# Seven products of halves in place of eight in the second product of the last dense layer

## Chip, core and metric

The kernel runs on one core of one Trainium2 chip. The metric is the device time of one execution in microseconds, the median of several runs; smaller is better. The engines are named as in the profile: PE is TensorE (matrix products, with PEld for the load of the stationary operand), DVE is VectorE, ACT is ScalarE, POOL is GpSimd, and SP is SyncE, which only issues DMAs here.

## What is computed

A trunk of two pre-norm residual layers over 512 tokens of width 1024, in float32. The first layer mixes tokens with a gated MLP over chunks, the second with multi-scale retention. Each is followed by a dense layer with squared ReLU, and a last RMSNorm ends the trunk. What matters here is the dense layer behind the second mixer and the norm at the end:

```python
h = rmsnorm(x, norm_ffn_g[i])
a = jax.nn.relu(h @ w1)            # 512 x 1024 times 1024 x 4096
x = x + (a * a) @ w2               # 512 x 4096 times 4096 x 1024
...
return rmsnorm(x, final_norm_g)
```

## The kernel before

**Precision.** Every float32 operand of a product is split in two fp32r parts, a high part (a cast, by ScalarE) and a low part (operand minus high part, by VectorE). A product is then three matmuls: high x high, high x low, low x high. `mm3` (L213 to L217) issues them; a line of it stands for matmuls of many places, so the profile's rows are told apart by their tiles: `up` is the first product of a dense layer, `dt` the second product of the last layer, `dn` that of the first.

**Weights.** `pieces_f` and `pieces_t` cut a weight matrix into raw tiles of 1 MB (`Raw`), each of which gives two pieces (`Piece`). `load_raws` (L160) issues the loads on SP into one of two raw buffers, `prep` (L172) splits a piece: ScalarE casts it to `wH` (L179, 4 buffers), VectorE subtracts to `wL` (L183, 3 buffers).

**Order.** The program is written out by hand: each engine executes its instructions in the order in which the code issues them (`manual_schedule`), and semaphores between engines follow from the tiles. `step` appends a step and the pieces that it uses to a list. At the end the list is run; each step issues its matmuls, then `advance` (the next part of unfinished evacuations, which are generators in `pending`), then `refill` (L199): high parts up to 3 pieces ahead of the step, low parts up to 2. Then come what the step has been given to do `behind` it and its own evacuation.

**Buffers.** A pool `bigp` of 10 buffers of 8 KB a partition holds the large activations. PSUM has 6 banks `acc` and 2 banks `mis`. The residual `xT` (features x tokens, 8 tiles) and the split normalised activations `hH`, `hL` have tiles of their own.

**The last dense layer.** The hidden width of 4096 is cut in four blocks q of 1024. `up(1, q)` (L641) computes one block of the first product in 8 steps (`feat`, L312), each 128 hidden features x 512 tokens, 8 row chunks x 3 = 24 matmuls with 512 columns. Its evacuation `evac_a` (L621) makes Relu and its square on ScalarE, and from them the split activations `aH`, `aL`. The norm's factor per token is not applied to the activations; its square, `r2`, is applied later. `down_t(q)` (L920) multiplies one block with w2: for each half c of the 1024 output columns four steps (`tokens`, L339), each 4 token tiles x 2 row chunks x 3 = 24 matmuls, accumulated in four PSUM banks over the block. `evac_last` (L861) adds a bank times `r2` to `xtok`, the residual with tokens on the partitions, which `to_tokens` (L847) makes by transposes during `up(1, 0)`. For the last block, `ends` (L897) goes token tile by token tile, so that the final norm and the stores (`finish`, L873) overlap. The order is up 0, gain load, up 1, down 0, up 2, down 1, up 3, down 2, down 3; `load_gain` (L929) loads the last norm's gain into `wide` and scales it.

**The norm ahead of it.** `norm` (L294) sums squares over features with a matmul by ones and forms the inverse root `r4` (`stats`); with `wide=True` it also spreads the factor over the partitions, by two more matmuls (`spread`, L281, rows `bc`), into `rbc`. The last layer's norm has `wide=False` before.

Of the kernel before, what the change touches and what calls it, by code (L numbers as in the profile page):

```python
# [32 lines left out]
class Raw:  # L33


    def __init__(self, src, parts=1):
        self.src, self.parts, self.tile, self.done = src, parts, None, 0


class Piece:  # L40
# [38 lines left out]
def trunk(ctx, tc, x, norm_mix_g, norm_ffn_g, a_w_in, a_b_in, a_v_norm_g, a_w_s, a_b_s, a_w_out,  # L79
          b_w_in, b_head_norm_g, b_w_out, mlp_w1, mlp_w2, final_norm_g, trig, decay, out):  # L80
    nc = tc.nc
    ctx.enter_context(tc.manual_schedule())

    keep = ctx.enter_context(tc.tile_pool(name="keep", bufs=1))
    wts = ctx.enter_context(tc.tile_pool(name="wts", bufs=3))
    bigp = ctx.enter_context(tc.tile_pool(name="bigp", bufs=10))
    work = ctx.enter_context(tc.tile_pool(name="work", bufs=2))
    psum = ctx.enter_context(tc.tile_pool(name="psum", bufs=6, space=PSUM))

    RAW_BUFS, LOOK = 2, 3  # L90

    def big(shape, dt, name):
        return bigp.tile(shape, dt, tag="big", name=name)

    def tmp(name, tag, bufs=2):
        return work.tile([P, T], F32, tag=tag, name=name, bufs=bufs)

    def zt(name):
        return tmp(name, "z", 4)
# [4 lines left out]
    def acc(name):  # L104
        return psum.tile([P, 512], F32, tag="acc", name=name, bufs=6)
# [4 lines left out]
    def f32(ap):  # L110
        return ap.bitcast(F32)
# [7 lines left out]
    wide = keep.tile([P, D], F32, name="wide")  # L119
    rbc, r2bc = wide[:, 0:T], wide[:, T:D]  # L120
# [7 lines left out]
    ms0 = keep.tile([P, NT], F32, name="ms0")  # L128

    keep.tile([P, 320], F32, name="fill")  # L130
    xT = [keep.tile([P, T], F32, name=f"xT{k}") for k in range(KD)]
    hH = [keep.tile([P, T], F32R, name=f"hH{k}") for k in range(KD)]
    hL = [keep.tile([P, T], F32R, name=f"hL{k}") for k in range(KD)]
    make_identity(nc, ident)
# [14 lines left out]
    order, steps, raws, pending = [], [], [], []  # L149
    pos = {"raw": 0, "piece": 0, "low": 0, "done": 0}  # L150

    def load_part(r):
        if r.tile is None:
            r.tile = wts.tile([P] + list(r.src.shape[1:]), F32, tag="raw", name=f"raw{raws.index(r)}", bufs=RAW_BUFS)
        s = r.src.shape[1] // r.parts
        i = r.done
        nc.sync.dma_start(out=r.tile[:, i * s : (i + 1) * s, :], in_=r.src[:, i * s : (i + 1) * s, :])
        r.done += 1

    def load_raws(upto):  # L160
        while pos["raw"] < min(upto, len(raws)):
            r = raws[pos["raw"]]
            while r.done < r.parts:
                load_part(r)
            pos["raw"] += 1

    def prep_tiles(i):
        p = order[i]
        p.hi = wts.tile(p.shape, F32R, tag="wH", name=f"wH{i}", bufs=4)
        p.lo = wts.tile(p.shape, F32R, tag="wL", name=f"wL{i}", bufs=3)  # L170

    def prep(upto, low=None):  # L172

        low = upto if low is None else low
        while pos["piece"] < min(upto, len(order)):
            p = order[pos["piece"]]
            load_raws(raws.index(p.raw) + RAW_BUFS)
            prep_tiles(pos["piece"])
            nc.scalar.copy(out=p.hi, in_=p.raw.tile[p.view])  # L179
            pos["piece"] += 1  # L180
        while pos["low"] < min(low, len(order)):
            p = order[pos["low"]]
            nc.vector.tensor_sub(out=p.lo, in0=p.raw.tile[p.view], in1=f32(p.hi))  # L183
            pos["low"] += 1

    def launch(g):
        if next(g, "end") != "end":
            pending.append(g)

    def advance():  # L190
        for g in list(pending):
            if next(g, "end") == "end":
                pending.remove(g)
# [5 lines left out]
    def refill():  # L199
        n = pos["done"]  # L200
        prep(n + (LOOK if n >= 4 else 1), n + (LOOK - 1 if n >= 4 else 1))

    def step(fn, *ps):
        for p in ps:
            order.append(p)
            if p.raw not in raws:
                raws.append(p.raw)
        steps.append((fn, ps))

    def do(fn):  # L210
        step(lambda: fn())

    def mm3(ps, ah, al, bh, bl, start, stop):  # L213

        nc.tensor.matmul(ps, lhsT=ah, rhs=bh, start=start, stop=False)  # L215
        nc.tensor.matmul(ps, lhsT=ah, rhs=bl, start=False, stop=False)  # L216
        nc.tensor.matmul(ps, lhsT=al, rhs=bh, start=False, stop=stop)  # L217


    state = {}  # L220
# [73 lines left out]
    def norm(name, wide=True, square=False):  # L294

        yield from stats(state["ssq"], r4, 1.0 / D, name)
        if wide:
            yield from spread(r4, rbc, name)
            if square:
                nc.scalar.activation(r2bc, rbc, AF.Square)  # L300


    def mm_f(p, ps, bH, bL, ks, last):
        for k in ks:
            mm3(ps, p.hi[:, k, :], p.lo[:, k, :], bH[k], bL[k], k == 0, k == last)
# [6 lines left out]
    def feat(p, bufs, evac, name, behind=None):  # L312

        def run(p):
            ps = acc(name)
# [211 lines left out]
    def nxt(g, times=1):  # L527
        return lambda: [next(g, None) for _ in range(times)]
# [92 lines left out]
    def evac_a(q, i):  # L621
        def ev(ps):
            b = 2 * q + i // 4
            if i % 4 == 0:
                aH[b] = big([P, 4, T], F32R, f"aH{q}_{i}")
                aL[b] = big([P, 4, T], F32R, f"aL{q}_{i}")
            h, l = aH[b][:, i % 4, :], aL[b][:, i % 4, :]
            r, s = zt(f"r{i}"), z2t(f"rr{i}")
            nc.scalar.activation(r, ps, AF.Relu)  # L629
            nc.scalar.activation(s, r, AF.Square)  # L630
            nc.vector.tensor_mul(h, r, r)  # L631
            yield
            nc.vector.tensor_sub(out=l, in0=s, in1=f32(h))
        return ev
# [210 lines left out]
    xtok = [None, None]  # L845

    def to_tokens(c, n):  # L847
        if n == 0:
            xtok[c] = big([P, NT, 512], F32, f"xtok{c}")
        ps = mis(f"tt{c}{n}")  # L850
        for k in range(4):
            nc.tensor.transpose(ps[:, k * P : (k + 1) * P], xT[4 * c + k][:, n * P : (n + 1) * P], ident)
        nc.scalar.copy(out=xtok[c][:, n, :], in_=ps)

    nrm_f1 = norm("ffn1", wide=False)

    def s2():
        next(nrm_f1, None)
        nc.vector.tensor_mul(r2, r4, r4)
# [67 lines left out]
    up(1, 0, {i: (lambda v=v, i=i: ([to_tokens(*a) for a in v], next(nrm_f1) if i == 2 else s2() if i == 3 else None)) for i, v in tt.items()}, late=True)  # L927

    def load_gain():  # L929
        nc.sync.dma_start(out=wide, in_=final_norm_g.partition_broadcast(P))  # L930
        nc.vector.tensor_scalar_mul(wide, wide, 0.125)

    do(load_gain)
    up(1, 1)
    down_t(0)
    up(1, 2)
    down_t(1)
    up(1, 3)
    down_t(2)
    down_t(3)  # L940


# [18 lines left out]
    for k in range(2):  # L961
        p = order[0]
# [56 lines left out]
```

## Time and profile before

| | |
|---|---|
| median of 3 runs | 1407.23 us (1405.75 to 1407.27) |
| the profiled execution's own time | 1407.72 us |
| its span, first to last instruction | 1406.0 us |
| PE busy | 1390.5 us, 6290 matmuls |
| DVE busy | 793.0 us, 1102 instructions |
| ACT busy | 507.2 us, 721 instructions |
| POOL busy | 127.7 us, 98 instructions |
| moved by DMA | 135.23 MB, mean 96 GB/s |
| mean granted PE clock | 0.998 |
| first matmul of the last dense layer | about 1043 us |
| last matmul of the kernel starts | 1395.26 us |

In a row of groups stand line, engine, operation, tiles out<-in and shape, the count, the busy time in us and the mean of one in ns, and behind the second bar the idle time of that engine just before these instructions, with what ended it. In a row of waits stand the waiting engine, tile and line, what released it, and the total, the number of times and the longest, in us. In a row of the timeline stand start and duration in us, and in square brackets the idle time before with its releaser.

### The profile page before, as it was taken

How to read it: one execution, taken by the hardware profiler on the slowest of the kernel's cores; microseconds unless marked ns; L12 is line 12 of the kernel's file. 1: busy time of each engine (PE TensorE's matmuls, PEld its weight loads, DVE VectorE, ACT ScalarE, POOL GpSimd, SP SyncE). 2: the span in 40 equal slices, each digit the busy share in tenths (PEclk: the TensorE clock that was granted, in tenths of full speed). 3: DMA queues.
4: the chain of work that ended last, by engine and by line, in shares of the span. 5: the costliest groups of instructions: out<-in, count | busy, mean ns of one | idle time of the engine just before them, and what ended most of it. 6: DMA issues, size and time to landing. Idle time of an engine off the chain costs nothing.

```text
span 1406.0 us, 15372 instructions
## 1 busy us (share of the span) xinstructions
PE 1390.5 (99%) x6290; PEld 1155.4 (82%) x6290; DVE 793.0 (56%) x1102; ACT 507.2 (36%) x721; POOL 127.7 (9%) x98
## 2 busy tenths in 40 slices
PE   8999999999999999999999999999999999999997
PEld 7888888888888888888888888888888888888885
DVE  6757765775444445476647574564685443434335
ACT  4656633334413223123334323333334422313222
POOL 3010111220000000011111100110130000000002
PEclk9999999999999999999999999999999999999999
DMA  6332222232223322423222131132122332232221
GB/s 225 109 116 90 72 90 88 81 120 90 90 90 104 106 90 90 148 89 108 90 78 72 60 120 60 62 118 90 61 90 91 120 104 90 93 117 91 90 90 60
DMA packets 106101, 135.23 MB, mean 96 GB/s; under 512 B 2400, under 2 KB 79792, under 8 KB 105776
## 3 DMA queue, kind: packets, MB, share of 16 engines
q1 hardware_dynamic: 106000, 134.26, 29.4%
q8 instruction: 49, 0.80, 0.2%
q14 instruction: 20, 0.16, 0.0%
q10 hardware_dynamic: 32, 0.01, 0.0%
HBM read 132.16 MB, written 2.10 MB: 95 GB/s over the span
## 4 chain that ended last, share of the span: by engine, by line
PE 96%; DVE 3%; POOL 0%; ACT 0%; DMA 0%; issue 0%; SPq 0%; ACTq 0%; DVEq 0%
PE up L217 8%; PE up L216 8%; PE up L215 8%; PE dn L217 4%; PE dn L216 4%; PE dn L215 4%; PE dt L216 4%; PE dt L217 4%; PE dt L215 4%; PE g L215 2%; PE qk L215 2%; PE vv L216 2%; PE g L216 2%; PE vv L215 2%; PE g L217 2%; PE vv L217 2%
## 5 line engine op out<-in xcount | busy, mean ns | idle before, releaser
L183 DVE TENSOR_TENSOR wL<-raw,wH 128x1024 fp32r<-128x1024 f32 x239 | 305.9, 1282 | 112.8 <-PE dt L216 65.5
L179 ACT CAST wH<-raw 128x1024 fp32r<-128x1024 f32 x239 | 249.7, 1045 | 264.7 <-PE dt L217 114.9
L215 PE MATMUL up<-hH,wH 128*128 128x512 f32 x480 | 187.2, 390 | 0.0
L217 PE MATMUL up<-hH,wL 128*128 128x512 f32 x480 | 186.8, 389 | 0.0
L216 PE MATMUL up<-hL,wH 128*128 128x512 f32 x480 | 186.8, 389 | 0.0
L631 DVE TENSOR_TENSOR aH<-r 128x512 fp32r<-128x512 f32 x64 | 45.0, 703 | 159.5 <-ACT r L629 159.4
L216 PEld LDWEIGHTS up<-hL,wH 128*128 128x128 f32 x480 | 90.1, 188 | 18.7
L215 PEld LDWEIGHTS up<-hH,wH 128*128 128x128 f32 x480 | 90.1, 188 | 18.7
L217 PEld LDWEIGHTS up<-hH,wL 128*128 128x128 f32 x480 | 90.1, 188 | 18.7
L215 PE MATMUL dn<-aH,wH 128*128 128x512 f32 x256 | 99.6, 389 | 0.0
L216 PE MATMUL dn<-aL,wH 128*128 128x512 f32 x256 | 99.6, 389 | 0.0
L217 PE MATMUL dn<-aH,wL 128*128 128x512 f32 x256 | 99.6, 389 | 0.0
L215 PE MATMUL dt<-wH,aH 128*128 128x512 f32 x256 | 99.6, 389 | 0.0
L216 PE MATMUL dt<-wL,aH 128*128 128x512 f32 x256 | 99.6, 389 | 0.0
L217 PE MATMUL dt<-wH,aL 128*128 128x512 f32 x256 | 99.6, 389 | 0.0
L629 ACT ACTIVATE r<-up 128x512 f32<-128x512 f32 x60 | 35.9, 598 | 166.7 <-PE up L217 166.7
L239 POOL TENSOR_TENSOR ssq<-ssq,sq 128x512 f32<-128x512 f32 x28 | 43.0, 1537 | 401.6 <-ACT sq L238 401.3
L501 DVE TENSOR_TENSOR xs<-dn,wide 128x512 f32<-128x512 f32 x32 | 22.1, 692 | 74.5 <-PE dn L217 74.5
L215 PEld LDWEIGHTS dt<-wH,aH 128*128 128x128 f32 x256 | 48.0, 188 | 10.1
L216 PEld LDWEIGHTS dn<-aL,wH 128*128 128x128 f32 x256 | 48.0, 188 | 10.0
L215 PEld LDWEIGHTS dn<-aH,wH 128*128 128x128 f32 x256 | 48.0, 188 | 10.0
L216 PEld LDWEIGHTS dt<-wL,aH 128*128 128x128 f32 x256 | 48.0, 188 | 9.9
(271 smaller groups left out, 2709.5 us busy)
## 6 DMA issues: line engine op xcount, KB each, us to landing
raw<-in_mlp_w_dram SPq DMA_DIRECT2D x64, 1024.0 KB, 5.1
raw<-in_b_w_in_dram SPq DMA_DIRECT2D x24, 1024.0 KB, 5.0
raw<-in_a_w_in_dram SPq DMA_DIRECT2D x14, 1024.0 KB, 5.2
raw<-in_a_w_out_dram SPq DMA_DIRECT2D x8, 1024.0 KB, 4.9
raw<-in_b_w_out_dram SPq DMA_DIRECT2D x8, 1024.0 KB, 4.9
raw<-in_a_w_in_dram SPq DMA_DIRECT2D x8, 256.0 KB, 6.7
out_dram<-out SPq DMA_DIRECT2D x8, 256.0 KB, 2.1
xr<-in_x_dram SPq DMA_DIRECT2D x3, 512.0 KB, 6.6
```

What stands on the lines that cost most here:

```text
L179: nc.scalar.copy(out=p.hi, in_=p.raw.tile[p.view])
L183: nc.vector.tensor_sub(out=p.lo, in0=p.raw.tile[p.view], in1=f32(p.hi))
L215: nc.tensor.matmul(ps, lhsT=ah, rhs=bh, start=start, stop=False)
L216: nc.tensor.matmul(ps, lhsT=ah, rhs=bl, start=False, stop=False)
L217: nc.tensor.matmul(ps, lhsT=al, rhs=bh, start=False, stop=stop)
L239: nc.gpsimd.tensor_tensor(out=state["ssq"], in0=state["ssq"], in1=sq, op=ALU.add)
L501: nc.vector.tensor_mul(t, ps, r2bc)
L629: nc.scalar.activation(r, ps, AF.Relu)
L631: nc.vector.tensor_mul(h, r, r)
```

## The change

The second product of blocks 0, 1 and 2 is done by seven products of halves (Strassen's scheme) in place of eight. With A the block's activations (512 tokens x 1024 features) and W its weights (1024 x 1024), both are cut into 2 x 2 quarters. Each of the seven products multiplies a quarter of A, or a sum of quarters (256 tokens x 512 features), with a quarter of W, or a sum of quarters (512 x 512). Its two token tiles are added to or subtracted from quarters of `xtok`, by VectorE straight from PSUM; where a product belongs to two quarters of the result, its bank is not cleared and the next product is accumulated on top (`BANK`, `FIRST`, `OUT`).

- `evac_n` replaces `evac_a` for these blocks: the factor `rbc` is applied before the square (so the norm has `wide=True`, and evacuations before the factor is there wait with Relu alone), and one float32 tile `aF` is kept unsplit.
- `make(s)` forms the activations' sum for product s where there is one (VectorE, into temporary tiles), casts it (ScalarE) and makes the low part (VectorE), into a tile `sp`. It is issued behind the first step of product s - 1.
- Sums of weights are formed by DMA: the first quarter is loaded on SP, and POOL issues a DMA that adds another quarter to the tile (`accum_op`). Three of the sums share one tile, `t1`, `t2`, `t4`: the next quarter is added when both pieces of the sum before are split (`over`, `split`). Per block that is 5 loads and 4 accumulating DMAs of 1 MB, where before there were 4 loads.
- The products of block q stand between the steps of `up` of block q + 1: one step of 24 matmuls, then one product (two steps of 12 matmuls). These `up` steps use the banks `mis`, the products the six banks `acc`.
- `load_gain` moves behind the last `up`, since `rbc` lies in `wide`. Block 3 keeps `down_t(3)`.
- Raw tiles and the residual move into `bigp`, which has 14 buffers now; loads run 2 raw tiles ahead as before, and 4 from the last dense layer on.

```diff
-    def __init__(self, src, parts=1):
+    def __init__(self, src, parts=1, adds=(), over=None):
         self.src, self.parts, self.tile, self.done = src, parts, None, 0
+        self.adds, self.over, self.split = adds, over, 0
...
-    bigp = ctx.enter_context(tc.tile_pool(name="bigp", bufs=10))
+    bigp = ctx.enter_context(tc.tile_pool(name="bigp", bufs=14))
...
-    RAW_BUFS, LOOK = 2, 3
+    LOOK = 3
+    ahead = {"raws": 2}
...
-    xT = [keep.tile([P, T], F32, name=f"xT{k}") for k in range(KD)]
+    xT2 = [big([P, 4, T], F32, f"xT{b}") for b in range(2)]
+    xT = [xT2[k // 4][:, k % 4, :] for k in range(KD)]
...
-            r.tile = wts.tile([P] + list(r.src.shape[1:]), F32, tag="raw", name=f"raw{raws.index(r)}", bufs=RAW_BUFS)
+            r.tile = big([P] + list(r.src.shape[1:]), F32, f"raw{raws.index(r)}")
...
             r = raws[pos["raw"]]
+            if r.over is not None:
+                if r.over.split < 2:
+                    return
+                r.tile, r.done = r.over.tile, r.parts
             while r.done < r.parts:
                 load_part(r)
+            for src in r.adds:
+                nc.gpsimd.dma_start(out=r.tile, in_=src, accum_op=ALU.add)
...
-            load_raws(raws.index(p.raw) + RAW_BUFS)
+            load_raws(raws.index(p.raw) + ahead["raws"])
...
             nc.vector.tensor_sub(out=p.lo, in0=p.raw.tile[p.view], in1=f32(p.hi))
+            p.raw.split += 1
             pos["low"] += 1
+            load_raws(raws.index(p.raw) + ahead["raws"])
...
-    nrm_f1 = norm("ffn1", wide=False)
+    nrm_f1 = norm("ffn1")
...
+    def evac_n(q, i):
+        def ev(ps):
+            b = 2 * q + i // 4
+            if i % 4 == 0:
+                aF[b] = big([P, 4, T], F32, f"aF{q}_{i}")
+            a = aF[b][:, i % 4, :]
+            if "rbc" in state:
+                r = zt(f"r{i}")
+                nc.vector.scalar_tensor_tensor(out=r, in0=ps, scalar=0.0, in1=rbc, op0=ALU.max, op1=ALU.mult)
+                nc.scalar.activation(a, r, AF.Square)
+                return
+            nc.scalar.activation(a, ps, AF.Relu)
+            while "rbc" not in state:
+                yield
+            nc.vector.tensor_mul(a, a, rbc)
+            nc.scalar.activation(a, a, AF.Square)
+            yield
+        return ev
+
+    def seven(q):
...
+        t1 = Raw(part(0, 0), adds=[part(0, 1)])
+        t2 = Raw(part(1, 1), adds=[part(1, 1)], over=t1)
+        t4 = Raw(part(1, 0), adds=[part(1, 0)], over=t2)
+        wraws = [Raw(part(0, 0)), t1, Raw(part(1, 0)), t2, Raw(part(1, 1)), Raw(part(0, 1), adds=[part(1, 1)]), t4]
...
+        def make(s):
+            def src(c):
+                if s in (0, 2, 6):
+                    return block(*((0, lo_t), None, (1, lo_t), None, None, None, (1, hi_t))[s], c)
+                if s == 1:
+                    sums["s", c] = half(tmp(f"sa{q}{c}", "uz"))
+                    nc.vector.tensor_sub(out=sums["s", c], in0=block(0, hi_t, c), in1=block(1, hi_t, c))
+                elif s == 3:
+                    nc.vector.tensor_sub(out=sums["s", c], in0=sums["s", c], in1=block(0, lo_t, c))
+                elif s == 4:
+                    nc.vector.tensor_add(out=sums["s", c], in0=sums["s", c], in1=block(1, lo_t, c))
+                else:
+                    sums["d", c] = half(tmp(f"sd{q}{c}", "sq"))
+                    nc.vector.tensor_sub(out=sums["d", c], in0=block(0, lo_t, c), in1=block(0, hi_t, c))
+                    return sums["d", c]
+                return sums["s", c]
+            sp = parts[s] = big([P, 2, 4, T // 2], F32R, f"sp{q}{s}")
+            for c in range(2):
+                v = src(c)
+                hi, lo = sp[:, 0, 2 * c : 2 * c + 2, :], sp[:, 1, 2 * c : 2 * c + 2, :]
+                nc.scalar.copy(out=hi, in_=v)
+                nc.vector.tensor_sub(out=lo, in0=v, in1=f32(hi))
+
+        BANK = "acbacaa"
+        FIRST = (0, 1, 2)
...
+        def one(s, i):
+            def run(p):
...
+                for t in range(2):
+                    ts = slice(t * P, (t + 1) * P)
+                    for k in range(2):
+                        kk = 2 * i + k
+                        mm3(banks[bk][t], sp[:, 0, kk, ts], sp[:, 1, kk, ts], p.hi[:, k, :], p.lo[:, k, :], s in FIRST and kk == 0, kk == 3, True)
+                advance()
+                refill()
+                if i == 0 and s < 6:
+                    make(s + 1)
+                if i == 1:
+                    (m, n), op = OUT[s]
+                    for t in range(2):
+                        xv = xtok[n][:, 2 * m + t, :]
+                        nc.vector.tensor_tensor(out=xv, in0=xv, in1=banks[bk][t], op=op)
...
+    do(lambda: ahead.update(raws=4))
...
+    for q in range(3):
+        pl = pieces_f(mlp_w1[1], (0, D), (1024 * (q + 1), 1024 * (q + 2)))
+        first, products = seven(q)
+        do(first)
+        for i in range(8):
+            feat(pl[i], hs, evac_n(q + 1, i) if q < 2 else evac_a(3, i), f"up1{q + 1}_{i}", bank=mis)
+            if i < 7:
+                products[i]()
     do(load_gain)
-    up(1, 1)
-    down_t(0)
-    up(1, 2)
-    down_t(1)
-    up(1, 3)
-    down_t(2)
     down_t(3)
```

More of the change, by code (lines that the diff above doesn't have):

```diff
@@ L211, in do, with mm3 @@
         step(lambda: fn())
[L213 to L217, printed above, removed]
+    def mm3(ps, ah, al, bh, bl, start, stop, resumed=False):
+        for i, (a, b) in enumerate(((ah, bh), (ah, bl), (al, bh))):
+            nc.tensor.matmul(ps, lhsT=a, rhs=b, start=start and i == 0, stop=stop and i == 2, skip_group_check=resumed)
     state = {}
@@ L310, in mm_o, with feat @@
             mm3(ps, p.hi[:, k, ts], p.lo[:, k, ts], bH[:, k, :], bL[:, k, :], k == 0, k == 3)
-    def feat(p, bufs, evac, name, behind=None):
+    def feat(p, bufs, evac, name, behind=None, bank=acc):
         def run(p):
-            ps = acc(name)
+            ps = bank(name)
             mm_f(p, ps, *bufs(), range(8), 7)
@@ L924, in down_t @@
                    last=ends if q == 3 and c == 1 else None)
-    tt = {2: [(0, 0), (0, 1)], 3: [(0, 2)], 4: [(0, 3)], 5: [(1, 0)], 6: [(1, 1)], 7: [(1, 2), (1, 3)]}
-    up(1, 0, {i: (lambda v=v, i=i: ([to_tokens(*a) for a in v], next(nrm_f1) if i == 2 else s2() if i == 3 else None)) for i, v in tt.items()}, late=True)
+    aF = {}
+    def evac_n(q, i):
[16 more added lines that the diff above has]
+        return ev
@@ new lines, in seven, with part, block, half @@
+    def seven(q):
+        w = mlp_w2[1]
+        def part(i, j):
+            r, c = 1024 * q + 512 * i, 512 * j
+            return w[r : r + 512, c : c + 512].rearrange("(k p) n -> p k n", p=P)
+        t1 = Raw(part(0, 0), adds=[part(0, 1)])
+        t2 = Raw(part(1, 1), adds=[part(1, 1)], over=t1)
+        t4 = Raw(part(1, 0), adds=[part(1, 0)], over=t2)
+        wraws = [Raw(part(0, 0)), t1, Raw(part(1, 0)), t2, Raw(part(1, 1)), Raw(part(0, 1), adds=[part(1, 1)]), t4]
+        pl = [[Piece(r, (slice(None), slice(2 * i, 2 * i + 2), slice(None)), [P, 2, 512]) for i in range(2)] for r in wraws]
+        lo_t, hi_t = slice(0, T // 2), slice(T // 2, T)
+        sums, parts, banks = {}, {}, {}
+        def block(h, ts, c):
+            return aF[2 * q + h][:, 2 * c : 2 * c + 2, ts]
+        def half(v):
+            return v.rearrange("p (k t) -> p k t", t=T // 2)
+        def make(s):
[22 more added lines that the diff above has]
+        FIRST = (0, 1, 2)
+        OUT = [((0, 0), ALU.add), ((1, 1), ALU.add), ((0, 0), ALU.add), ((0, 1), ALU.subtract), ((0, 1), ALU.add), ((1, 1), ALU.subtract), ((1, 0), ALU.add)]
+        def one(s, i):
+            def run(p):
+                bk = BANK[s]
+                if i == 0 and s in FIRST:
+                    banks[bk] = [acc(f"sm{q}{bk}{t}") for t in range(2)]
+                sp = parts[s]
+                for t in range(2):
[12 more added lines that the diff above has]
+                        nc.vector.tensor_tensor(out=xv, in0=xv, in1=banks[bk][t], op=op)
+            return run
+        return (lambda: make(0)), [lambda s=s: [step(one(s, i), pl[s][i]) for i in range(2)] for s in range(7)]
@@ L929, in load_gain, with got_rbc, behind_up0 @@
+    def got_rbc():
+        next(nrm_f1, None)
+        state["rbc"] = True
+    tt = {2: [(0, 0), (0, 1)], 3: [(0, 2)], 4: [(0, 3)], 5: [(1, 0)], 6: [(1, 1)], 7: [(1, 2), (1, 3)]}
+    norms = {2: nxt(nrm_f1), 3: s2, 4: nxt(nrm_f1), 5: got_rbc}
+    def behind_up0(i):
+        for a in tt.get(i, []):
+            to_tokens(*a)
+        if i in norms:
+            norms[i]()
     def load_gain():
@@ L931, in load_gain @@
         nc.vector.tensor_scalar_mul(wide, wide, 0.125)
-    do(load_gain)
-    up(1, 1)
-    down_t(0)
-    up(1, 2)
-    down_t(1)
-    up(1, 3)
-    down_t(2)
+    pl = pieces_f(mlp_w1[1], (0, D), (0, 1024))
+    do(lambda: ahead.update(raws=4))
+    feat_late(pl[0], pl[1], (evac_n(0, 0), evac_n(0, 1)), "up10")
+    for i in range(2, 8):
+        feat(pl[i], hs, evac_n(0, i), f"up10_{i}", lambda i=i: behind_up0(i))
+    for q in range(3):
[6 more added lines that the diff above has]
+                products[i]()
+    do(load_gain)
     down_t(3)
```

## Prediction

> **What bounds the kernel now.** I read first the busy table and the shares of the chain that ended last, then the waits of TensorE over the whole span, then the last stage in the timeline.
>
> ```profile
> PE 1390.5 (99%) x6290; PEld 1155.4 (82%) x6290; DVE 793.0 (56%) x1102; ACT 507.2 (36%) x721; POOL 127.7 (9%) x98
> PE 96%; DVE 3%; POOL 0%; ACT 0%; DMA 0%; issue 0%; SPq 0%; ACTq 0%; DVEq 0%
> ```
> ```profile
> engine line waited for: us in total, times, longest us
> PE xt L397 <- DMA xr<-in_x_dram: 1.8, 1, 1.8
> PE warm L958 <- POOL ident masks.py:199: 1.4, 1, 1.4
> PE bc_h L290 <- DVE dg_h L286: 0.9, 3, 0.3
> PE st_mix L272 <- POOL st_mix L263: 0.9, 1, 0.9
> ```
>
> TensorE is busy for 1390.5 of 1406.0 us, and all its waits add up to 5.0 us, none of them in the last dense layer. The remaining 10.5 us are the tail behind its last matmul. So the time moves with the number of matmuls and their spacing, as long as nothing makes TensorE wait. The spacing, from matmuls of the second product:
>
> ```profile
> 1160.20 0.39 PE L215 MATMUL dt<-wH,aH 128*128 128x512 f32 x1
> ...
> 1162.92 0.39 PE L215 MATMUL dt<-wH,aH 128*128 128x512 f32 x1
> ```
> ```profile
> L215 PE MATMUL dt<-wH,aH 128*128 128x512 f32 x256 | 99.6, 389 | 0.0
> L215 PE MATMUL up<-hH,wH 128*128 128x512 f32 x192 | 74.8, 389 | 0.0
> ```
>
> Between the two quoted starts lie 12 matmuls in 2.72 us: 0.2267 us each (0.39 is the pipelined duration, not the cost). The groups of the window 1090:1400 show `up` and `dt` at the same 389 ns, with no idle time. A step of 24 matmuls is 5.44 us, one of 12 is 2.72 us.
>
> The other engines run ahead of TensorE in this stage:
>
> ```profile
> L183 DVE TENSOR_TENSOR wL<-raw,wH 128x1024 fp32r<-128x1024 f32 x54 | 67.1, 1242 | 79.0 <-PE dt L216 65.5 <-issue 13.5
> L179 ACT CAST wH<-raw 128x1024 fp32r<-128x1024 f32 x53 | 55.5, 1047 | 114.9 <-PE dt L217 114.9
> ```
> ```profile
> 1091.00:1180.00 89.00, 89.00 (x394) 73.67 (x394) 38.83 (x44) 28.56 (x37) 0.00 (x0) 1.00 0.34 109
> 1110.00:1120.00 10.00, 10.00 (x46) 8.29 (x45) 4.16 (x6) 3.90 (x6) 0.00 (x0) 1.00 0.33 107
> ```
>
> The weight splits wait for TensorE to free their buffers, not the other way. The second fence is the table by stretches (PE, PEld, DVE, ACT, POOL busy; clock; DMA share; GB/s): VectorE is busy for 44% of 1091:1180, ScalarE for 32%, the DMA engines for a third, POOL not at all, and the clock is full.
>
> **The matmuls.** Before, each of the three blocks is 8 steps of 24 matmuls: 192. After, it is 7 products of 2 steps, each step 2 token tiles x 2 row chunks x 3 terms = 12 matmuls: 168. Three blocks save 72 matmuls, 72 x 0.2267 = **16.3 us**. The free size stays 512, and each matmul still loads its own stationary tile, so I keep the spacing. Added are the two matmuls that spread the norm's factor (`bc`); before runs the same pair without a visible price in the first dense layer, here 2 x 0.23 = **0.5 us**, up to 0.9 if they wait as `bc_h` does. Net 15.8 us, if the rest stays hidden.
>
> **VectorE, the engine that could become the bound.** A weight split now serves 12 matmuls instead of 24, and the sums and splits of the activations come on top. The prices:
>
> ```profile
> L864 DVE SCALAR_TENSOR_TENSOR xtok<-dt,r,xtok 128x512 f32<-128x512 f32 x32 | 24.0, 750 | 20.2 <-PE dt L217 20.2
> L633 DVE TENSOR_TENSOR aL<-rr,aH 128x512 fp32r<-128x512 f32 x25 | 17.3, 693 | 2.8 <-DVE aH L631 0.5
> L629 ACT ACTIVATE r<-up 128x512 f32<-128x512 f32 x25 | 15.0, 599 | 79.4 <-PE up L217 79.4
> ```
> ```profile
> L504 DVE TENSOR_TENSOR xT<-xT,ro 128x512 f32<-128x512 f32 x3 | 2.0, 677 | 0.0
> ```
> ```profile
> L788 ACT CAST ryH<-o 128x512 fp32r<-128x512 f32 x16 | 9.8, 622 | 18.8 <-DVE o L787 18.8
> ```
>
> One step of `up` and one product form a group of 5.44 + 2 x 2.72 = 10.88 us of TensorE. VectorE's work in a heavy one (the next product needs a sum): 3 weight splits x 1.22 (the 67.1 us above without one slow split of 2.34, quoted below, over 53), the evacuation of `up` 0.75, two sums and two low parts x 0.69, two updates of `xtok` x 0.68 (L504 also adds PSUM into SBUF): 8.5 us. In program order each low part directly follows its ScalarE cast, so VectorE waits out two casts x 0.62: 9.8 of 10.88 us. Written out from the start of `up` at 0: evacuation 5.60 to 6.35 (it has to wait for the end of `up`); split of the next `up` to 7.57, due 10.88; sums, casts and low parts to 11.57, due 16.32; split of the next product's first piece to 12.79, due 16.32; updates of `xtok` to 14.15, due 16.32 in the one case where the next product uses the same bank (sixth to seventh); split of the second piece to 15.37, due 19.04. The next evacuation is ready at 16.48, so 1.1 us stay idle and the pattern repeats. The smallest margin is 2.2 us. In the third block `up` still makes split activations: the evacuation begins after Relu and is 2 x 0.69; the last split ends at 16.60 where the next evacuation can begin at 17.08, and margins are 2.1 us and more. Of the six preparations inside a block, four are heavy. The sums run over two stretches of 256 instead of one of 512, which no row shows; at 10% more it is 0.3 us a group, inside the idle 1.1. So I cost this at **nothing**; the cover is the group's TensorE time, and beyond a margin of about 2 us a delay of VectorE turns into waits of TensorE.
>
> **The accumulating DMAs.** Four per block, 1 MB each, issued by POOL; t1 = W00 + W01 is loaded, then added to, then split, and t2 and t4 are added into the same tile after its splits. No DMA of before accumulates, and none of the large ones is issued by POOL. The nearest rows:
>
> ```profile
> raw<-in_mlp_w_dram SPq DMA_DIRECT2D x64, 1024.0 KB, 5.1
> raw<-in_a_w_in_dram SPq DMA_DIRECT2D x8, 256.0 KB, 6.7
> wide<-in_final_norm_g_dram SPq DMA_DIRECT2D x1, 512.0 KB, 6.0
> ```
>
> Lower bound 5.1 us, the plain load. Upper bound 4 x 6.7 = 26.8 us, had a megabyte come as four 256 KB pieces one after another. In 1110:1120 a third of the DMA time moves 107 GB/s, so 1.05 MB streams in 1.05 / (107 / 0.33) = 3.2 us; an accumulate also has to fetch the tile, so I take 5.1 + 3.2 = 8.3 us, near the plain load, since bytes, rows and target are the same. When is it late? t2 can start when VectorE has split t1's second piece, about 2.7 us into the second `up` (13.6 us from the block's start); its product starts at 38.1, and 5.6 us go for what is queued behind the waiting ScalarE cast (1.05, then two casts x 0.62 and three sums and low parts x 0.69 of the fourth product's activations, and the split's 1.22), for which TensorE waits: 18.9 us are there. On POOL, which has no other work between the norm and the tail, t2, then W01 + W11, then t4 queue behind one another: t4 has to be ready at 65, so three in a row from 13.6 leave **17 us** for each. At 8.3 us there is twice what is needed: cost **nothing**. The DMA engines carry 9 plain loads x 3.2 and 4 accumulates x 6.4 us in a block of 81.6: 67% (plain alone would be 36%). Plain loads are issued up to four tiles ahead instead of two.
>
> **What is moved.** The gain vector's load and scaling go from the start to behind the last `up`. VectorE waits at worst 6.0 us for the load (2.0 before), and behind it stand the last low part and the split that TensorE needs 10.88 us later: nothing. The last block now begins directly behind its `up`; the chunks just evacuated are needed only in its fourth step, 16 us on: nothing. The residual tiles and the raw weights move into one pool of 14 buffers; before had 10, 2 and room for the residual, so the capacity is the same, and SP's loads wait for whichever buffer is free. TensorE's slack there is unknown: nothing, up to one step late (rival C). The tail is untouched.
>
> **Sum.** Span 1406.0 - 16.3 + 0.5 = 1390.2. The profiled run took 1407.72, 1.7 more than its span, and is 0.5 above the median 1407.23; so 1391.9 against that run, and **1391.4** against the median.
>
> **Rivals.**
>
> A, nothing waits: 1390 to 1394. For it: every due time above is met.
>
> B, POOL holds up VectorE. In the tail the two meet:
>
> ```profile
> 1376.35 1.30 POOL L869 TENSOR_TENSOR xtok<-xtok,wide 128x512 f32<-128x512 f32 x1 [0.36 <-ACT fsq L866]
> 1376.39 2.34 DVE L183 TENSOR_TENSOR wL<-raw,wH 128x1024 fp32r<-128x1024 f32 x1
> ```
> ```profile
> L420 POOL TENSOR_SCALAR ws<-ws 128x1024 f32<-128x1024 f32 x1 | 2.8, 2776 | 1.9 <-DMA ws<-in_a_b_s_dram 1.9
> ```
>
> The split took 2.34 us beside a 1.30 us POOL instruction, 1.22 elsewhere. If POOL's work for an issue does the same for d us, each of 12 accumulates costs TensorE d - 2.2 (the margin): nothing at 1.3, 0.6 at 2.8 (POOL's longest row quoted), so 7 us: 1398. At d = 3.5 the gain is gone. I give it 1394 to 1404. Against it: nothing shows that issuing a DMA behaves like a POOL addition. [...]
>
> C, the common pool delays loads:
>
> ```profile
> SPq L157 <- DVE wL L183: 311.0, 30, 12.7
> ```
>
> SP already waits for VectorE to free raw tiles, up to 12.7 us at a time in 1040:1406; a load behind a tile that TensorE frees later could leave TensorE one step short: 1391.4 + 5.4 = 1397.
>
> D, slower: the accumulates are late. Place: POOL's chain of four a block. Above 17 us each they begin to delay TensorE; at 4 x X > 81.6, X > 20.4, they set the pace; the 15.8 us are gone at X = (81.6 + 5.3) / 4 = 21.7 us. At the upper bound 26.8 the blocks take 107.2 us: 3 x 25.6 = 77 more, 1468. Against it: that is over four plain loads; for it: no row shows one.
>
> **Chances.** A 0.57; B 0.17, of which 0.02 loses the whole gain to within 0.2%; C 0.06; D 0.15, of which 0.02 near no change; 0.05 for a delay in something that I took as unaffected, slower. 0.2% (2.8 us) is about what a measurement of this kernel can tell from no change. Faster 0.57 + 0.15 + 0.06 = 0.78; within 0.2% 0.04; slower 0.13 + 0.05 = 0.18. The range 1390 to 1405 takes in A, B and C, 0.80; D is left out.
>
> **What would show it.** A: 6220 matmuls, TensorE at 0.227 us, waits of TensorE still near 5 us, VectorE 80% busy inside the blocks. B: the weight splits' mean above 1.3 us and TensorE waiting for them. C: TensorE waiting for `wL` before 1040. D: an accumulate's time to landing above 17 us, ScalarE's casts of raw waiting for a DMA, and lines of TensorE waiting in the fourth and seventh product. If the spacing of matmuls in the products is not 0.227 us, the first term is wrong: each 1% of it over the 576 + 504 matmuls of the three blocks is 2.4 us.

## The result and the profile after

The changed kernel takes 1392.24 us (median of 4 runs, 1390.86 to 1393.44) against 1406.95 us of before on the same chip: ratio 0.9897, 95% interval 0.9880 to 0.9914. The profiled execution took 1392.35 us with a span of 1390.6 us. 1391.4 was forecast, with a span of 1390.2.

The busy table and the chain's shares by engine, after:

```profile
PE 1374.3 (99%) x6220; PEld 1142.2 (82%) x6220; DVE 845.8 (61%) x1183; ACT 536.2 (39%) x764; POOL 143.8 (10%) x110
PE 95%; DVE 3%; POOL 1%; DMA 0%; ACT 0%; issue 0%; SPq 0%; ACTq 0%; DVEq 0%; POOLq 0%
```

The waits of TensorE over the whole span, after:

```profile
engine line waited for: us in total, times, longest us
PE xt L408 <- DMA xr<-in_x_dram: 1.8, 1, 1.8
PE warm L1091 <- POOL ident masks.py:199: 1.4, 1, 1.4
PE bc_h L301 <- DVE dg_h L297: 0.9, 3, 0.3
PE st_mix L283 <- POOL st_mix L274: 0.8, 1, 0.8
PE st_mix L282 <- ACT st_mix L273: 0.3, 1, 0.3
PE up L228 <- ACT xtok L864: 0.2, 1, 0.2
```

TensorE has 70 matmuls fewer and 16.2 us less of busy time. Its waits sum to 5.4 us (5.0 before), and of the last dense layer there is one of 0.2 us among them. VectorE has 53 us more to do, ScalarE 29, and none of it shows in TensorE's waits. The kernel is bound as before, by a shorter list of matmuls.

One heavy group of the first block, VectorE's timeline (start, duration, instruction, idle time before it):

```profile
1140.60 0.69 DVE L956 SCALAR_TENSOR_TENSOR r<-up,wide 128x512 f32<-128x512 f32 x1 [1.63 <-PE up L228]
1141.21 1.22 DVE L193 TENSOR_TENSOR wL<-raw,wH 128x1024 fp32r<-128x1024 f32 x1
1142.35 0.68 DVE L1003 TENSOR_TENSOR sd<-aF 128x512 f32<-128x512 f32 x1
1143.71 0.69 DVE L1012 TENSOR_TENSOR sp<-sd,sp 128x512 fp32r<-128x512 f32 x1 [0.69 <-ACT sp L1011]
1144.33 0.68 DVE L1003 TENSOR_TENSOR sd<-aF 128x512 f32<-128x512 f32 x1
1145.69 0.69 DVE L1012 TENSOR_TENSOR sp<-sd,sp 128x512 fp32r<-128x512 f32 x1 [0.69 <-ACT sp L1011]
1146.31 1.22 DVE L193 TENSOR_TENSOR wL<-raw,wH 128x1024 fp32r<-128x1024 f32 x1
1147.44 1.27 DVE L1037 TENSOR_TENSOR xtok<-xtok,sm0c 128x512 f32<-128x512 f32 x2
1148.64 1.22 DVE L193 TENSOR_TENSOR wL<-raw,wH 128x1024 fp32r<-128x1024 f32 x1
1151.48 0.69 DVE L956 SCALAR_TENSOR_TENSOR r<-up,wide 128x512 f32<-128x512 f32 x1 [1.63 <-PE up L228]
```

This is the group that the prediction wrote out by hand. From one evacuation of `up` to the next it is 10.88 us, TensorE's time; VectorE waits out two ScalarE casts at 0.69 each and at the end waits 1.63 us for TensorE. As long as that last wait is there, VectorE is not the bound.

The table by stretches, one row for each of the three blocks (PE, PEld, DVE, ACT, POOL busy; clock, DMA share, GB/s):

```profile
1090.99:1172.60 81.61, 81.37 (x360) 67.33 (x360) 52.66 (x65) 35.07 (x46) 5.14 (x4) 1.00 0.70 181
1172.60:1254.20 81.60, 81.60 (x362) 67.59 (x361) 53.36 (x66) 34.43 (x44) 5.15 (x4) 1.00 0.63 155
1254.20:1335.80 81.60, 81.60 (x362) 67.59 (x361) 57.86 (x73) 38.62 (x51) 3.87 (x3) 1.00 0.52 136
```

A block lasts 81.6 us, as worked out. The accumulating DMAs, in the table of issues (KB each, median us from issue to landing) and in that of the queues (packets, MB, share of 16 engines):

```profile
raw<-in_mlp_w_dram SPq DMA_DIRECT2D x67, 1024.0 KB, 5.2
raw<-in_mlp_w_dram POOLq DMA_DIRECT2D x12, 1024.0 KB, 8.9
```
```profile
q1 hardware_dynamic: 107584, 137.41, 29.9%
q0 software_dynamic: 6336, 12.58, 5.4%
```

An accumulate lands after 8.9 us where a plain load takes 5.2. Per MB it occupies the DMA engines for 0.054 x 1390.6 / 12.58 = 6.0 us, a load for 0.299 x 1390.6 / 137.41 = 3.0 us: twice.

### The profile page after: what moved, and what is told of

It reads as the page before. It is cut to its first block, busy times and chain, and to the rows that moved or that the text cites. A ratio compares the mean times of both kernels' runs of the same rounds, so it can differ in the third digit from the quotient of the medians.

```text
span 1390.6 us, 15387 instructions
## 1 busy us (share of the span) xinstructions
PE 1374.3 (99%) x6220; PEld 1142.2 (82%) x6220; DVE 845.8 (61%) x1183; ACT 536.2 (39%) x764; POOL 143.8 (10%) x110
## 3 DMA queue, kind: packets, MB, share of 16 engines
q1 hardware_dynamic: 107584, 137.41, 29.9%
q0 software_dynamic: 6336, 12.58, 5.4%
## 4 chain that ended last, share of the span: by engine, by line
PE 95%; DVE 3%; POOL 1%; DMA 0%; ACT 0%; issue 0%; SPq 0%; ACTq 0%; DVEq 0%; POOLq 0%
PE up L228 24%; PE dn L228 13%; PE g L228 6%; PE qk L228 6%; PE vv L228 6%; PE u L228 6%; PE o L228 6%; PE v L228 5%; PE ro L228 5%; PE dt L228 3%; PE av L228 2%; PE sm2a L228 2%; PE sm1a L228 2%; PE sm0a L228 2%; PE sc L228 1%; PE v L573 1%
## 5 line engine op out<-in xcount | busy, mean ns | idle before, releaser
L193 DVE TENSOR_TENSOR wL<-raw,wH 128x1024 fp32r<-128x1024 f32 x257 | 327.4, 1276 | 49.5 <-PE v L228 10.7
L189 ACT CAST wH<-raw 128x1024 fp32r<-128x1024 f32 x257 | 267.4, 1045 | 170.0 <-PE dn L228 101.1
L642 DVE TENSOR_TENSOR aH<-r 128x512 fp32r<-128x512 f32 x40 | 27.7, 692 | 94.5 <-ACT r L640 94.4
L250 POOL TENSOR_TENSOR ssq<-ssq,sq 128x512 f32<-128x512 f32 x28 | 43.5, 1555 | 400.8 <-ACT sq L249 400.5
L640 ACT ACTIVATE r<-up 128x512 f32<-128x512 f32 x38 | 22.7, 597 | 112.5 <-PE up L228 112.5
L228 PEld LDWEIGHTS dn<-aH,wL 128*128 128x128 f32 x256 | 48.1, 188 | 9.9
L228 PE MATMUL u<-hH,wH 128*128 128x512 f32 x128 | 50.6, 395 | 0.0
L228 PE MATMUL g<-hH,wH 128*128 128x512 f32 x128 | 50.5, 395 | 0.0
L228 PE MATMUL o<-yH,wH 128*128 128x512 f32 x128 | 50.4, 394 | 0.0
L228 PE MATMUL qk<-hH,wH 128*128 128x512 f32 x128 | 50.0, 391 | 0.0
```

What stands on the lines that cost most here:

```text
L228: nc.tensor.matmul(ps, lhsT=a, rhs=b, start=start and i == 0, stop=stop and i == 2, skip_group_check=resumed)
L250: nc.gpsimd.tensor_tensor(out=state["ssq"], in0=state["ssq"], in1=sq, op=ALU.add)
```

## The experiments

The theory: the time is the number of matmuls times 0.2267 us, and VectorE's work and the accumulates are hidden, each with a margin that can be measured. The rivals: part of the gain comes from the new order or the buffers; the accumulates or VectorE are not as well hidden as they look. All runs were compared with runs of before on their own chip, whose medians were 1406.8 to 1407.4 us; the changed kernel's 1392.24 was measured in a run of its own.

### Eight products instead of seven, all else kept

Each product takes plain quarters (activations' half, token half, column half in `USE`); one split quarter of the activations serves two products, and two products are accumulated in a bank.

```diff
-        wraws = [Raw(part(0, 0)), t1, Raw(part(1, 0)), t2, Raw(part(1, 1)), Raw(part(0, 1), adds=[part(1, 1)]), t4]
+        USE = [(0, 0, 0), (0, 0, 1), (1, 0, 0), (1, 0, 1), (0, 1, 0), (0, 1, 1), (1, 1, 0), (1, 1, 1)]
+        BANK = "ababcaca"
...
+              for r in [Raw(part(h, n)) for h, m, n in USE]]
...
-        BANK = "acbacaa"
...
-            if i < 7:
-                products[i]()
+            products[i]()
```

> The three blocks are done as eight products of quarters in place of seven: everything else of the change stays (interleaving with the steps of up, activations kept whole and split late, common buffer pool), but no sums and no accumulating DMAs. 72 matmuls more than the changed kernel, 6292 in all. Theory (the time is the count of matmuls x 0.2267 us, all else is hidden): 1392.2 + 16.3 = 1408.5 us, span 1406.9, waits of TensorE near 5 us. Rival (the interleaving or the new buffers bring part of the gain): clearly below 1406.9, the time of before.

Measured: 1408.43 us (1406.78 to 1409.72), ratio to before 1.0009 (0.9999 to 1.0018), span 1406.7, TensorE busy 1391.2 us with 6292 matmuls. 16.2 us are given back, to the forecast within 0.1. The order, the late split and the norm's spread factor bring nothing; the count brings all.

### Two blocks instead of three

```diff
-    for q in range(3):
+    for q in range(2):
...
-            feat(pl[i], hs, evac_n(q + 1, i) if q < 2 else evac_a(3, i), f"up1{q + 1}_{i}", bank=mis)
+            feat(pl[i], hs, evac_n(q + 1, i) if q < 1 else evac_a(2, i), f"up1{q + 1}_{i}", bank=mis)
...
     do(load_gain)
+    up(1, 3)
+    down_t(2)
     down_t(3)
```

> Only blocks 0 and 1 are done by seven products; block 2 and 3 by the old steps. 24 matmuls more than the changed kernel. Theory (count): a third of the gain is given back, 1392.2 + 5.4 = 1397.7 us. Rival (the blocks differ: the third, where up still splits its activations, costs VectorE most and brings less than the others): below 1397.

Measured: 1397.26 us (1396.48 to 1397.77), 0.9930 (0.9915 to 0.9945). 5.0 us are given back for 24 matmuls (5.4 by the count, and the medians of the two runs scatter by about 1 us). Whether the third block brings a little less than the others can't be told from this.

### Four blocks

The fourth block's products stand alone behind the last `up`; the gain is scaled behind the second of them; the tail (`square_up` and `both`: squares, gain and `finish`, as in `evac_last` and `ends`) is done per token tile as its quarters are complete.

```diff
+                    if q == 3:
+                        if s in (2, 4, 5, 6):
+                            for t in range(2):
+                                square_up(2 * m + t, n)
+                        if s in (4, 6):
+                            both(2 * m, 2 * m + 1)
...
-            feat(pl[i], hs, evac_n(q + 1, i) if q < 2 else evac_a(3, i), f"up1{q + 1}_{i}", bank=mis)
+            feat(pl[i], hs, evac_n(q + 1, i), f"up1{q + 1}_{i}", bank=mis)
...
     do(load_gain)
-    down_t(3)
+    first, products = seven(3)
+    do(first)
+    for i in range(7):
+        products[i]()
+        if i == 1:
+            do(scale_gain)
```

> All four blocks by seven products; behind the last up there is nothing to place between the products of block 3, and the final norm and the stores follow the token tiles as they are finished. 24 matmuls fewer than the changed kernel. Theory (the cover of VectorE's work is the up step between the products): a product alone is 5.4 us of TensorE but 7.4 us of VectorE where a sum is needed, 5.3 otherwise, so seven take about 46 us and 3 us at the start, with some 5 us of final norm on VectorE between them, against 43.5 us now, and the tail has two token tiles instead of one: 1400 to 1408 us, TensorE waiting for low parts by VectorE. Rival (the count alone decides): 1392.2 - 5.4 = 1386.8 us.

Measured: 1410.17 us (1409.36 to 1411.38), 1.0025 (1.0015 to 1.0034), the slower side of before in spite of 94 matmuls fewer (four times 24, less the two that spread the factor), and 2 us above the range that I had given. The waits of TensorE in the last block, and below them one of ScalarE:

```profile
PE sm3a L228 <- DVE xtok L1037: 8.3, 1, 8.3
PE sm3a L228 <- ACT sp L1011: 6.1, 3, 3.3
PE sm3c L228 <- ACT sp L1011: 1.2, 1, 1.2
```
```profile
ACT wH L189 <- DMA raw<-in_mlp_w_dram: 8.0, 1, 8.0
```

From the end of the last `up` (1336.6) to the start of the last matmul (1396.84) it is 60 us, where `down_t(3)` takes 43.5. The seven products alone would be 38.1 us; TensorE's waits between them sum to 16.5 us, and its busy time is 6 us above the count, at a granted clock of 0.88 in 1360:1370, 0.82 in 1380:1390 and 0.84 in 1390:1400. Without an `up` step between the products VectorE's groups are longer than TensorE's (7.4 us from 1357.41 to 1364.84, against 5.4 us of matmuls), the final norm of the first two token tiles stands on VectorE for 5 us behind the fifth product's updates, so that the sixth's come late and the seventh waits for its bank, and, which I had not counted, the second sum of weights is late: ScalarE waits 8.0 us for its accumulate. The `up` steps are the cover of both.

### The common buffer pool alone

```diff
-    bigp = ctx.enter_context(tc.tile_pool(name="bigp", bufs=10))
+    bigp = ctx.enter_context(tc.tile_pool(name="bigp", bufs=14))
...
-    xT = [keep.tile([P, T], F32, name=f"xT{k}") for k in range(KD)]
+    xT2 = [big([P, 4, T], F32, f"xT{b}") for b in range(2)]
+    xT = [xT2[k // 4][:, k % 4, :] for k in range(KD)]
...
-            r.tile = wts.tile([P] + list(r.src.shape[1:]), F32, tag="raw", name=f"raw{raws.index(r)}", bufs=RAW_BUFS)
+            r.tile = big([P] + list(r.src.shape[1:]), F32, f"raw{raws.index(r)}")
```

> The kernel before with one part of the change alone: raw weights and residual in the common pool of 14 buffers. Theory (the place of the buffers costs and brings nothing): 1406 to 1408 us, waits of TensorE near 5 us as before. Rival (the common pool delays loads, rival C of the prediction): above 1410 us with TensorE waiting for wL before the last layer. A gain below 1404 us would mean that part of the change's gain comes from here.

Measured: 1407.29 us (1406.64 to 1408.79), 1.0002 (0.9993 to 1.0012). Nothing gained or lost; rival C falls.

### No accumulates

```diff
-            for src in r.adds:
-                nc.gpsimd.dma_start(out=r.tile, in_=src, accum_op=ALU.add)
```

> The changed kernel without its twelve accumulating DMAs: each sum of weights is only its first quarter, so the products are not those of the reference. Theory (the accumulates are hidden): no change, 1391 to 1393.5 us. Rival (they hold VectorE or the loads up by a little everywhere): lower, 1390.5 or less, with the span nearer to the 1390.2 of the sum.

Measured: 1391.70 us (1391.21 to 1392.52), 0.9888 (0.9873 to 0.9902), span 1389.9. That is 0.5 us below the changed kernel, with ranges that overlap: the twelve accumulates cost at most about that.

### Each accumulate twice, and three times

```diff
-            for src in r.adds:
+            for src in r.adds * 2:
```

> Each quarter is added twice, the second addition waiting for the first, so a sum of weights takes two accumulates of 8.9 us one after another, some 18.5 us (the sums are not those of the reference). In the changed kernel the second sum's accumulate is issued 15.7 us into a block and its cast is due at about 32.5 us. Theory (due times): late by 0 to 2 us per block, 1392 to 1398 us, ScalarE waiting for the DMA ahead of the fourth product only. Rival (the accumulates never matter, loads are far enough ahead): 1392. Rival (POOL's issues and the traffic hold up VectorE): over 1400.

> Each quarter is added three times, one after another, some 27.5 us for a sum of weights (the sums are not those of the reference); this is the upper bound that the prediction gave to one accumulate. Theory (due times): the second sum late by about 11 us and the third by about 6 more in each block, 3 x 17 = 51 us: about 1443 us, more than before. Prediction's own figure for this case (POOL's chain of four sets the pace): 1468. Rival (hidden anyway): 1392.

(`r.adds * 3` for three.)

Measured: twice 1401.31 us (1399.30 to 1404.72), 0.9958 (0.9943 to 0.9973); three times 1495.32 us (1494.59 to 1496.55), 1.0622 (1.0604 to 1.0639). Both are later than my due times gave (0 to 6 and 51 us more; 9 and 103 were measured). TensorE's waits in the three blocks, with two additions and with three:

```profile
PE sm2a L228 <- DVE wL L193: 2.5, 1, 2.5
PE sm1a L228 <- DVE xtok L1037: 2.2, 1, 2.2
PE sm0a L228 <- DVE xtok L1037: 2.1, 1, 2.1
...
PE sm1a L228 <- DVE wL L193: 0.8, 1, 0.8
```
```profile
PE sm1a L228 <- DVE xtok L1037: 19.1, 1, 19.1
PE sm0a L228 <- DVE xtok L1037: 18.1, 1, 18.1
PE sm2a L228 <- DVE xtok L1037: 16.4, 1, 16.4
PE sm1a L228 <- ACT sp L1011: 8.2, 1, 8.2
PE sm0a L228 <- ACT sp L1011: 7.9, 1, 7.9
PE sm2a L228 <- ACT sp L1011: 7.6, 1, 7.6
...
```

By their times in the trace they stand where the due times put them: ahead of the fourth product, which needs the second sum, and of the seventh, which needs the last, but for one of 1.3 us ahead of the sixth. (The rows with `xtok` are the seventh's: VectorE's update of the bank stands in its order behind the low part that waits for ScalarE's casts.) With two additions the waits sum to 7.6 us and TensorE's busy time grows by 1.7: together the 9. With three they sum to 87.6 us, and the busy time grows by 16.2 at a lower granted clock (0.966 over the span, 0.997 in the changed kernel): together the 104 by which the span grew.

With three, the fourth product is 7.9 + 3.0 us late in the first block, as the 11 of the expectation. What the due times missed is the last sum, 18 us late instead of 6, and the clock. The issues of its three additions on POOL (the second of the first pair, the single one, the first of the last pair), and ScalarE's cast of the finished sum:

```profile
1150.32 2.59 POOL L174 DMA_DIRECT2D raw<-in_mlp_w_dram  x2 [7.84 <-DMA raw<-in_mlp_w_dram]
1168.89 1.28 POOL L174 DMA_DIRECT2D raw<-in_mlp_w_dram  x1 [15.97 <-DMA raw<-in_mlp_w_dram]
1181.89 2.59 POOL L174 DMA_DIRECT2D raw<-in_mlp_w_dram  x2 [11.72 <-DMA raw<-in_mlp_w_dram]
...
1190.62 1.04 ACT L189 CAST wH<-raw 128x1024 fp32r<-128x1024 f32 x1 [20.76 <-DMA raw<-in_mlp_w_dram]
```

The issues wait on one another in POOL's order: behind the two issued together at 1150.32 POOL waited 16.0 us, behind the single one ahead of them 7.8. From 1151.6 to 1190.6 this sum takes 39 us instead of the 27.5 that I had put in.

Rival D's pace, POOL's four sums against a block of 81.6 us, does not show. The second sum is issued behind the start of its block's first product, here in the second block of the changed kernel and of the run with three additions:

```profile
1178.48 0.39 PE L228 MATMUL sm1a<-wH,sp 128*128 128x512 f32 x1
...
1188.23 2.58 POOL L174 DMA_DIRECT2D raw<-in_mlp_w_dram  x2 [38.70 <-DVE wL L193]
```
```profile
1213.66 0.39 PE L228 MATMUL sm1a<-wH,sp 128*128 128x512 f32 x1
...
1223.91 1.30 POOL L174 DMA_DIRECT2D raw<-in_mlp_w_dram  x1 [17.05 <-DVE wL L193]
```

That is 9.8 us in the one and 10.3 in the other (9.8 with two additions), so POOL still begins each block in time, and TensorE does not wait for the first sum, whose product uses the banks `c`. What is borne out is D's other threshold, 17 us a sum: with two additions the last sum is ready 53.4 us after the issue of the second in the first block (1106.72 to 1160.1), three times 17.8, and TensorE waits 2.1 us for it. One accumulate a sum is far below it.

### Loads two ahead instead of four

```diff
-    do(lambda: ahead.update(raws=4))
```

> The changed kernel with loads only two raw tiles ahead in the last layer, as in the rest of the kernel. Theory (due times): the accumulates are issued later, the last sum of a block about 54 us into it, ready at about 65, when it is due: hidden or late by 1 to 2 us per block, 1392 to 1398 us. Rival (the lead of four is what hides them): 1400 or more.

Measured: 1391.75 us (1391.60 to 1391.97), 0.9888 (0.9873 to 0.9902), no different from four ahead. In its trace the second sum of the three blocks is still issued at 1106.26, 1187.85 and 1270.88 (1106.65, 1188.23 and 1271.26 with four). The longer lead hides nothing that was not hidden.

### More work on VectorE

```diff
-    keep.tile([P, 320], F32, name="fill")
+    fill = keep.tile([P, 320], F32, name="fill")
+    nc.gpsimd.memset(fill, 0.0)
...
+                    for _ in range(4):
+                        nc.vector.tensor_add(out=fill, in0=fill, in1=fill)
```

(`range(10)` for ten.)

> The changed kernel with four additions of 128 x 320 on a scratch tile by VectorE behind each preparation of a product (six in a block), about 0.35 us each, 1.4 us a group. In the trace of the changed kernel VectorE is idle for 1.63 us in a heavy group of the first two blocks and 0.83 us in the third. Theory (that idle time is the cover): hidden, 1392 to 1394 us. Rival (VectorE already sets the pace in the groups): 18 x 1.4 = 25 us more, 1417.

> The same with ten additions, about 3.5 us a group. Theory: the four heavy groups of a block go 1.9 us (2.7 in the third block) beyond VectorE's idle time, of which 2 to 3 us a block are absorbed by the lead of the splits: 5 us in each of the first two blocks and 8 to 10 in the third, 1408 to 1414 us; TensorE waits for sp and wL by VectorE. Rival (VectorE is far from the bound): 1392. Rival (every added us counts): 18 x 3.5 = 63 us, 1455.

Measured: four 1394.03 us (1392.93 to 1394.34), 0.9906 (0.9890 to 0.9923); ten 1444.57 us (1442.38 to 1447.59), 1.0269 (1.0253 to 1.0286). Four came out as expected; ten is 30 us above my range of 1408 to 1414. One burst and the next in a heavy group of the first block, with ten:

```profile
1130.34 5.22 DVE L1035 TENSOR_TENSOR fill<-fill 128x320 f32<-128x320 f32 x10
...
1144.64 5.23 DVE L1035 TENSOR_TENSOR fill<-fill 128x320 f32<-128x320 f32 x10
```

An addition takes 0.52 us, not the 0.35 that I had put in, an estimate that no row shows (each reads what the one before wrote; whether that is the cause was not tried); four are 2.1 us a group, ten 5.2. The heavy group is then 1144.64 - 1130.34 = 14.3 us instead of 10.88, and VectorE does not wait for TensorE in it. With that price, put in after the run, the theory's sum is (5.2 - 1.63) x 4 heavy groups and (5.2 - 3.3) x 2 light ones (3.3 us idle there in the changed kernel's timeline), less 2 to 3 us of lead: 15 us a block, 20 in the third, 50 together; 52 were measured (in the profiled execution, 55 us longer, the blocks are 17.7, 17.7 and 20 us longer). Four additions go 0.4 us beyond the idle time in heavy groups of two blocks, which the lead takes, and 1.2 in the third: TensorE waits there for `wL` for 0.7 and 0.4 us, 1.8 us are lost. Both rivals fall: no loss at all (1392 with ten), and every added us lost, which at 0.52 us an addition would be 1429 and 1486 instead of the 1417 and 1455 on record: VectorE's margin is real and about as wide as its last wait in the group, 1.63 us.

## Why the prediction was right

- **The matmuls.** 16.3 us less, 0.5 for the two added: TensorE's busy time fell by 16.2, and giving the eighth product back cost 16.2. The spacing stayed at 0.2267 us: a block of 360 matmuls lasts 81.6 us.
- **VectorE.** Idle time of 1.1 us in a heavy group was worked out, and 0.5 in the third block; the trace has 1.63 and 0.83. The difference is that neighbouring instructions overlap (a split of 1.22 lets the next start after 1.14), which I had not taken off. My sign for it, "80% busy inside the blocks", was put wrongly: that holds for a heavy group (7.9 of 10 us in 1140:1150), the blocks as a whole are at 65% to 71%.
- **The accumulates.** 8.3 us were taken from bounds of 5.1 and 26.8; 8.9 were measured. That an accumulate also fetches the tile was part of the estimate, and no row of before shows it; measured is the DMA time a MB, 6.0 us against 3.0 for a load, where I had put 6.4 against 3.2. The DMA share of 67% a block was measured as 0.70, 0.63 and 0.52. The second sum is issued 15.7 us into its block, where 13.6 was worked out, so the 17 us left for a sum are rather 16.5. The time did not hang on how near 8.3 comes to 8.9: without the accumulates it is 0.5 us shorter, and with sums of about 18 us 9 us longer.
- **What was moved.** The pool brings no difference by itself. In the four-block kernel the next `up` as cover is missed at once, which is the statement "cover is TensorE's group" from the other side.
- **Rival B** (POOL's issue holds up VectorE). POOL is busy for 1.27 us an issue. Beside it the split keeps its 1.22 us, and the mean of all 66 in the blocks is 1217 ns; over the whole kernel it is 1276, and 1277 without the accumulates:

```profile
1148.26 1.27 POOL L174 DMA_DIRECT2D raw<-in_mlp_w_dram  x1 [18.60 <-DVE xtok L1037]
1148.64 1.22 DVE L193 TENSOR_TENSOR wL<-raw,wH 128x1024 fp32r<-128x1024 f32 x1
```
```profile
L193 DVE TENSOR_TENSOR wL<-raw,wH 128x1024 fp32r<-128x1024 f32 x66 | 80.3, 1217 | 1.4 <-ACT wH L189 1.4
```

  So POOL's issue did not slow this split, where in the tail of before one of the same size took 2.34 us beside a POOL addition of 1.30.
- **Rival D**: its condition was not met. Its first threshold, 17 us a sum, and its signs (TensorE waiting in the fourth and the seventh product, ScalarE's casts of raw waiting for a DMA) are what the runs with two and three additions show. Its price, (4 x X - 81.6) a block, is not shown: the loss with three additions is near it (28 us a block, 85 in three, at 27.5 us a sum; 88 us of waits and 103 in all were measured), but it comes from two late sums inside each block and from the lower clock, not from POOL's pace.
- **What was off.** The forecast is 0.8 us low. 0.4 of it is in the span (1390.6 against 1390.2): TensorE's waits are 0.4 longer, and behind the last matmul's start lie 1390.6 - 1379.54 = 11.1 us, 10.7 before; busy time fell by 0.4 more than forecast. The rest is within the scatter of the runs.

## What to carry to other kernels

Where the trace shows one engine busy from end to end and all others waiting for it, a smaller count of its instructions was worth its full price here (16.2 us for 72 matmuls at 0.2267), as far as every group of the new work still ended with the other engines waiting; writing out one group, with the waits between engines inside it, was enough to tell that here. Such cover belongs to a place: the same seven products without an `up` step between them cost more than the eight (60 us against 43.5 behind the last `up`). An engine's work put into a DMA was free here, to 0.5 us for twelve accumulates, as long as each result landed before the engine that reads it got there; room for the DMAs in the whole period was not enough: in the run with two additions their share was 0.82 in 1090:1190, 0.87 in 1190:1290 and 0.78 in 1290:1345, and 9 us were lost.

## What the runs showed of the hardware

- An accumulating DMA of 1 MB from HBM onto an SBUF tile took 8.9 us to land (median of twelve) and twice the DMA time of a load (6.0 against 3.0 us a MB); in the run with three additions POOL waited up to 16.3 us behind two issued together, and 7.8 behind the single one ahead of 1150.32.
- In the run with three additions the long waits cost TensorE more than themselves: they add up to 88 us, but the span grew by 104. Three stretches in and behind the last wait of the first block (TensorE busy, clock, DMA share, GB/s):

```profile
1180.00:1190.00 10.00, 0.00 (x0) 0.61 0.66 111
1190.00:1200.00 10.00, 4.61 (x12) 0.53 0.74 128
1200.00:1210.00 10.00, 10.00 (x45) 1.00 1.09 305
```

  The granted clock is at 0.53 where the matmuls begin again, and back at 1.00 in the next stretch. In the run with ten additions on VectorE the clock was 0.97 in 1090:1190, 0.97 in 1190:1290 and 0.93 in 1290:1390, with waits of 3.1, 3.1 and 3.9 us at the longest in the three blocks; with each accumulate twice it was 1.00 in 1090:1190, 1190:1290 and 1290:1345, with waits of 2.1, 2.2 and 2.5 us. How long a wait has to be before the clock is lower is not shown.
- An in-place chain of ten additions on VectorE took 5.22 us, 0.52 each, for 128 x 320 elements, three quarters of the 0.68 to 0.69 us of one on 128 x 512 for five eighths of the elements.
